# An inverse stored transposed, a gelu moved to its own projection, and deeper weight tiles in a hybrid encoder block

## The chip, the cores and the metric

The kernel runs on one core of a Trainium2 chip. A time is the device time of one execution in microseconds (us). The kernel before was run three times: 1186.85, 1188.13 and 1191.43 us, median 1188.13 us.

The core has engines with a queue each that they work through in order: TensorE (PE, matmuls and its weight loads), VectorE (DVE), ScalarE (ACT), GpSimd (POOL) and SyncE (SP, which only starts transfers here). They wait for each other through semaphores.

## The reference, cut to what matters

One layer of an encoder over 512 tokens with 1024 channels, all in float32: a norm, one wide projection, three branches that mix along the tokens, their gated sum, an output projection with a residual, and an MLP with squared relu between two more norms.

```python
h = rms_norm(x, norm1_g);  p = h @ w_in
y_a = b_a * causal_dwconv(c_a * x_a, conv_a_w)
u   = causal_dwconv(x_b, lru_conv_w, lru_conv_b)
y_b = rg_lru(u, ...) * gelu(g_b)                       # gelu in its tanh form
y_c = rwkv7_recurrence(r, decay, k, v, kk, a) ...      # 16 heads of 64, by token
m   = gate_a * y_a + gate_b * y_b + gate_c * y_c
x   = x + m @ w_out
x   = x + square(relu(rms_norm(x, norm2_g) @ mlp_w1)) @ mlp_w2
return rms_norm(x, final_g)
```

The recurrence of the third branch is worked in chunks of 64 tokens. For that, the inverse of a unit triangular 64x64 matrix is needed for each head and chunk: 16 x 8 = 128 inverses.

## The kernel before, in words

**Precision and the weight stream.** Each float32 operand of a large matmul is split into a high and a low half (float32r each), and three matmuls give the product: high by high, high by low, low by high (`mm3`, L153 to L155). Weights are streamed: `load_half` brings 128x512 values into a tile `raw` by a transfer on SP's queue, ACT casts them to `whi` (L131), and DVE subtracts that from `raw` into `wlo` (`tt`, recorded at L94). A weight block of 1024 rows is two such halves and feeds 24 matmuls, 12 for each half. There are 3 tiles `raw`, 4 `whi` and 4 `wlo`, so a load waits until a tile's last reader is done. Instructions recorded at L94, L97 and L100 belong to helpers (`tt`, `stt`, `ts2`) that the whole kernel uses; one tells them apart by tiles. The tiles of the work pools are shown by the first letters of their tags (`u1` to `u5` all as `u`, `g1` to `g3` as `g`), since numbers are left out.

**The order.** The third branch goes in four groups of four heads. For each group there is a critical chain: `amat` (products `pA`, masked into `AXt`), `inverse`, `chain` (the chunks one after the other) and `post`. Beside it run two fillers: `ab(q)`, the two other branches for a block of 128 channels (two blocks to a group), and `krv(g + 1)`, the inputs of the next group. `weave` hands out steps of the fillers between the yields of the critical part at fixed rates (`R0`, `P1`, `WPOST`, `R4`, `R5`). A list scheduler then orders the instructions of each engine when the program is built: by priority among those whose inputs and tiles are free by its own clock. The weight stream has the highest offset (`OFF` = 160), the critical chain 150 (`CP`), the inverse's tail 60 (`CPI`); the prologue has 20 and 30. On the chip, each engine then keeps that order.

**The inverse.** The diagonal blocks of 32x32 are inverted on DVE, 64 at a time, one per partition (partitions 64 to 127). Two transposes of 32x32 blocks (L482, one for each diagonal block) bring the masked matrix `AXt` into `la`; the identity is loaded into `xt` by a transfer on POOL's queue (L484). Then 31 steps follow, each a multiply into `tmp` and an add into `xt`, of (31 - s)(s + 1) elements. Both `la` and `xt` lie in the tile `Z`, `tmp` in the tile `dg`. Two more transposes (L499) bring the result into `TT`, also in `Z`, another one (L504) a copy into `dg`. After 16 empty yields, which leave the time to the filler, PE forms the off-diagonal block (`pG` at L509, `pT` at L517).

**The filler `ab(q)`.** It projects xb, gb, gatb and c, computes the gates of the linear recurrence from the convolution of xb (`pga`, `pgi`, which need its halves `uh` and `ul`), then the gelu of gb, the recurrence's scan, and projects x, b and ga. Its tiles `u1` to `u5` and `g1` to `g3` have one buffer each; the gelu's tile shares the tag `u3` with the input gate's, and the scaled gate (`gt`) shares `u5` with what follows the scan.

**Later stages.** The merged tiles of the first six blocks go to DRAM and come back on POOL's queue when the last inverse is done (`open_m`, L799 to L801). Then come the output projection (`acc`), and the MLP, whose first and second products have the stretch from 840 us on nearly to themselves.

Of the kernel before, what the change touches and what calls it, by code (L numbers as in the profile page):

```python
# [18 lines left out]
P = 128  # L19
# priorities of the weight stream, the prologue and the critical steps over what is emitted beside them  # L20
OFF, OFFS, OFFP = 160, 20, 30
CP, CPI, CPP = 150, 60, 30
# empty steps that leave the latency of an inverse, or of a norm, to the filler
NINV, NPOST = 16, 6
# steps of the fillers, and their shares by part of the critical path
N_AB, N_KRV = 28, 24
# [62 lines left out]
def block_kernel(ctx, tc, xt, win, par, mulr, sw, wout, w1, w2, fg, cst, eyes, out):  # L89
# [3 lines left out]
    def tt(o, a, b, op):  # L93
        return v.tensor_tensor(out=o, in0=a, in1=b, op=op)  # L94

    def stt(o, a, s, b, op0, op1):
        return v.scalar_tensor_tensor(out=o, in0=a, scalar=s, in1=b, op0=op0, op1=op1)  # L97
# [12 lines left out]

# [1 line left out]
    ident = cp.tile([P, P], F32, name="ident")  # L112
# [8 lines left out]

# [1 line left out]
    def load_w(src):  # L123
# [3 lines left out]
    def load_half(src, i):  # L127
        raw = wp.tile([P, S], F32, tag="raw", name="raw", bufs=3)
        sy.dma_start(raw, src[:, i * S:(i + 1) * S])
        hi = wp.tile([P, S], F32R, tag="whi", name="whi", bufs=4)  # L130
        ac.copy(hi, raw)  # L131
        lo = wp.tile([P, S], F32R, tag="wlo", name="wlo", bufs=4)
        tt(lo, raw, f(hi), SUB)
        return hi, lo
# [22 lines left out]
    def pin(first, mm):  # L157
        # in the order of the program, behind the matmuls before it
        if first:
            tc.keep_in_program_order(mm)  # L160

    def rsqrt(x, y, t):
        # Newton's steps from a first guess on the exponent; within 2 ulp after the third
        ts2(y.bitcast(I32), x.bitcast(I32), -0.5, RSQ, MUL, ADD)
        for _ in range(3):
            tt(t, x, y, MUL)
            stt(t, t, -0.5, y, MUL, MUL)
            stt(y, t, 1.5, y, ADD, MUL)

    def rsqrt_rows(pool, o, ps, low, scale=1.0):  # L170
        # rows alike in each 32: tokens to partitions, the root there, and back
        w = pool.tile([P, S], F32, tag="rqw", name="rqw")
        q = pool.tile([P, 3, 16], F32, tag="rqq", name="rqq")
        v.transpose(w, ps)
        wv = w.rearrange("p (b j) -> p b j", j=32)[:, :, 0]
        if scale == 1.0:
            v.tensor_scalar(out=q[:, 0], in0=wv, scalar1=low, scalar2=None, op0=MAX)
        else:
            ts2(q[:, 0], wv, scale, low, MUL, ADD)
        rsqrt(q[:, 0], q[:, 1], q[:, 2])  # L180
        v.transpose(o, q[:, 1].unsqueeze(2).to_broadcast([P, 16, 32]))

    # =======================================================================
    # projections and the three branches
    # =======================================================================
    ht_ctx = ExitStack()
# [102 lines left out]
    def W(tag, bufs=1):  # L289
        return wk.tile([P, S], F32, tag=tag, name=tag, bufs=bufs)  # L290
# [3 lines left out]

    # low-rank inputs, and the first key tile, on x before its norm's scale
    def unscaled(t, tag):
# [8 lines left out]

    # derived per-channel values
    # sigmoid(z) = (1 + tanh(z / 2)) / 2 throughout: tanh shares its table with exp
    for i, (n, c) in enumerate((("mu_k", -1.0), ("mu_r", -1.0), ("ka", -0.5), ("mu_v", -1.0))):
# [28 lines left out]

    # softplus of the recurrence's parameter
    apv = part[:, PI["ap"]]
# [32 lines left out]
    def krv(g, G_):  # L372
# [5 lines left out]
        for jj in range(2):  # L378
# [50 lines left out]
            tt(G_.BK[:, jj, :, 1], c3(kp), c3(pinv), MUL)  # L429
            # by head: the two tiles' halves side by side  # L430
            if jj == 0:
# [16 lines left out]
    def amat(G_):  # L448
        # A^T = [b|k]^T [a|r], masked
        G_.AX = sp.tile([P, 4, NC, 2, L], F32, tag="AXt", name="AXt")  # L450
        for jj in range(2):
            for c4 in range(2):
                pts = [pm.tile([P, 4, P], F32, tag="pm", name="pA") for h in range(2)]
                for ci in range(4):
                    c = 4 * c4 + ci
                    for h in range(2):
                        rows = slice(64 * h, 64 * h + 64)
                        pe.matmul(pts[h][:, ci], G_.BK[rows, jj, c], G_.AR[rows, jj, c],  # L458
                                  start=True, stop=True)
                for h in range(2):  # L460
                    tt(G_.AX[:, 2 * h + jj, 4 * c4:4 * c4 + 4].rearrange("p c a t -> p c (a t)"),
                       pts[h], mask.unsqueeze(1).to_broadcast([P, 4, P]), MUL)
                yield
        G_.BKT = sp.tile([P, NC, 2, P], F32, tag="BKT", name="BKT")
        for c2 in range(4):
            pt = pm.tile([P, 4, P], F32, tag="pm", name="pB")
            for i in range(4):
                c, jj = 2 * c2 + i // 2, i % 2
                pe.transpose(pt[:, i], G_.BK[:, jj, c].rearrange("p a t -> p (a t)"), ident)
            ac.copy(G_.BKT[:, 2 * c2:2 * c2 + 2].rearrange("p c j t -> p (c j) t"), pt)  # L470
            yield
        G_.RT = sp.tile([P, 2, NC, L], F32, tag="RT", name="RT")
        ac.copy(G_.RT, G_.AR[:, :, :, 1])

    def inverse(G_):
# [5 lines left out]
        for b in range(2):  # L481
            v.transpose(la[32 * b:32 * b + 32].rearrange("l s t -> l t s"),  # L482
                        AXt[32 * b:32 * b + 32, :, :, 0, 32 * b:32 * b + 32].rearrange("s e c t -> s t (e c)"))
        gp.dma_start(xt.rearrange("l s t -> l (s t)"), eyes)  # L484
        # xt[l, s, t] = X[t, s];  X[t, :] += A[t, s] X[s, :], la[l, s, t] = A[t, s]
        yield
        yield
        for s in range(31):
            n, c = 31 - s, s + 1
            tv = tmp[:, 0:n * c].rearrange("l (c t) -> l c t", c=c)  # L490
            tt(tv, la[:, s, s + 1:32].unsqueeze(1).to_broadcast([64, c, n]),
               xt[:, 0:c, s:s + 1].to_broadcast([64, c, n]), MUL)
            tt(xt[:, 0:c, s + 1:32], xt[:, 0:c, s + 1:32], tv, ADD)
            if s % 2 == 1:
                yield
        TT = Z[0:64].rearrange("p a b c -> p (a b c)").rearrange("p (l t) -> p l t", t=L)
        gp.memset(TT[32:64, :, 0:32], 0.0)
        for b in range(2):
            v.transpose(TT[32 * b:32 * b + 32, :, 32 * b:32 * b + 32].rearrange("s l t -> s t l"),  # L499
                        xt[32 * b:32 * b + 32].rearrange("l s t -> l t s"))  # L500
        for _ in range(NINV):
# [139 lines left out]
    def ab(q):  # L641
        # the recurrent branch, then the convolution's
        px = W("u2")
# [9 lines left out]
        t = yield from proj(("gb", q))  # L653
        ac.copy(gb, t)
        yield
        gt = W("u5")
        t = yield from proj(("gatb", q))
        ac.activation(gt, t, AF.Tanh, bias=pv("mgb", q), scale=0.5)
        stt(gt, gt, 1.0, gb, ADD, MUL)
        yield  # L660
        cs = W("g1")
# [15 lines left out]
        ac.activation(ga, ga, AF.Tanh, scale=dvp(P4, q), bias=dvp(P4, q))  # L677
        g2 = W("u3")
        ac.activation(g2, gb, AF.Square)
        ac.activation(g2, g2, AF.Copy, scale=0.044715, bias=1.0)  # L680
        tt(g2, g2, gb, MUL)
        ac.activation(g2, g2, AF.Tanh, scale=0.5 * GELU_C)
        stt(gb, g2, 1.0, gt, ADD, MUL)
        a2 = W("u5")
# [93 lines left out]
    for g in range(NG - 1):  # L778
        fl = fill_main(g)
        # steps of the two fillers, spread over 31 + 24 + 10 steps of the critical part  # L780
        nab = 2 * N_AB - (21 * R0 if g == 0 else 0)
        r2 = ((1 - P1) * nab + N_KRV) / (24 + 10 * WPOST)
        segments([(chainit(amat(GS[g]), inverse(GS[g])), P1 * nab / 31), (chain(GS[g], 0, NC), r2),
                  (post(g, GS[g]), WPOST * r2)], fl)
        drain(fl)

# [1 line left out]
    G_ = GS[NG - 1]  # L788
# [96 lines left out]

    # =======================================================================
    # MLP; the second norm's scale goes to its end
    # =======================================================================
    NA = 3 * NF // 4
    with tc.tile_pool(name="mw", bufs=2) as mw, \  # L890
# [34 lines left out]
        gp.memset(epst, EPS)  # L925
        # the square of the second norm's scale, by token
        sc2 = cp.tile([P, 4], F32, name="sc2")
# [127 lines left out]
```

## Time and profile before

| | |
|---|---|
| Runs | 1186.85, 1188.13, 1191.43 us |
| Profiled execution, span from first to last instruction | 1188.4 us |
| Mean granted TensorE clock | 0.985 |
| PE busy (modelled), matmuls | 1155.3 us (97%), 6396 |
| DVE busy, instructions | 786.9 us (66%), 1537 |
| ACT busy, instructions | 550.5 us (46%), 1005 |
| POOL busy, instructions | 59.2 us (5%), 99 |
| DVE's splits of weights (`wlo`) | 340 of 695 ns, 235.4 us |
| The inverse's 248 steps on DVE | 84.4 us |
| The chain that ended last | PE 84%, DVE 12% |

A row of instructions shows the start, the length, the engine, the line, the operation, the tiles it writes and reads, and the shapes; in brackets, the engine's idle time before it and what ended that. In a row of waits stand who waited, for whom, the total, the count and the longest. Matmuls overlap: the next starts before the one before it has ended, so the distance of their starts is their price. A granted clock of 0.50 means that PE ran at half speed.

### The profile page before, as it was taken

Reading aid. Unit: us, or ns where it says so; the run is one execution under the profiler, and the core shown is the slowest. Engines: PE = TensorE matmul, PEld = TensorE weight load, DVE = VectorE, ACT = ScalarE, POOL = GpSimd, SP = SyncE. Lnnn points to the kernel's source line nnn. Section 1 sums busy time; section 2 is a strip of 40 time slices with the busy share of each in tenths; the row PEclk is TensorE's granted clock in tenths of the full one; section 3 lists DMA queues with packets and bytes.
Section 4 is the critical chain, followed back from the end, with each engine's and each line's share of the span. In section 5 each row is a group of like instructions: output and inputs, shape, how many; then the busy total and the mean of one; then the engine's idle time right before and its main releaser. Section 6 shows DMA issues by size and latency. Waiting matters only on the chain.

```text
span 1188.4 us, 17270 instructions
## 1 busy us (share of the span) xinstructions
PE 1155.3 (97%) x6396; PEld 896.6 (75%) x6396; DVE 786.9 (66%) x1537; ACT 550.5 (46%) x1005; POOL 59.2 (5%) x99
## 2 busy tenths in 40 slices
PE   8999989999999999989999989999999999999996
PEld 4677876677777677767677766889888888888885
DVE  7997985689975678985688975677544444222225
ACT  6655364444556443565444545556444443222224
POOL 4100000000000000000000011000000000000003
PEclk9899988999999999999999999999999999999999
DMA  5231230222332122233122244436323333433322
GB/s 183 89 89 54 89 98 28 63 85 71 96 114 72 41 80 80 85 106 90 46 80 67 71 126 150 151 116 187 124 90 98 89 98 118 154 101 91 105 89 98
DMA packets 61973, 114.69 MB, mean 97 GB/s; under 512 B 7232, under 2 KB 10816, under 8 KB 61888
## 3 DMA queue, kind: packets, MB, share of 16 engines
q1 hardware_dynamic: 54960, 95.49, 26.2%
q0 software_dynamic: 6352, 17.30, 4.6%
q8 instruction: 50, 0.82, 0.3%
q10 hardware_dynamic: 576, 0.79, 0.2%
q14 instruction: 35, 0.29, 0.1%
HBM read 104.64 MB, written 8.91 MB: 96 GB/s over the span
## 4 chain that ended last, share of the span: by engine, by line
PE 84%; DVE 12%; issue 2%; ACT 1%; DMA 0%; SPq 0%; DVEq 0%; ACTq 0%
PE pp L153 12%; PE pp L155 11%; PE pp L154 11%; PE acc L153 6%; PE acc L154 6%; PE acc L155 6%; PE p L155 5%; PE p L153 5%; PE p L154 5%; DVE wlo L94 3%; PE py L582 2%; PE pA L458 2%; PE py L584 2%; DVE Z L94 2%; DVE dg L94 2%
## 5 line engine op out<-in xcount | busy, mean ns | idle before, releaser
L94 DVE TENSOR_TENSOR wlo<-raw,whi 128x512 fp32r<-128x512 f32 x340 | 235.4, 695 | 250.6 <-ACT whi L131 241.7
L131 ACT CAST whi<-raw 128x512 fp32r<-128x512 f32 x340 | 209.7, 619 | 379.1 <-PE acc L155 124.5
L155 PE MATMUL pp<-hh,wlo 128*128 128x512 f32 x696 | 284.4, 410 | 14.8 <-DVE wlo L94 14.5
L153 PE MATMUL pp<-hh,whi 128*128 128x512 f32 x696 | 285.0, 412 | 1.3 <-ACT hh L254 1.3
L154 PE MATMUL pp<-hl,whi 128*128 128x512 f32 x696 | 282.1, 407 | 3.1 <-DVE hl L97 3.1
L155 PEld LDWEIGHTS pp<-hh,wlo 128*128 128x128 f32 x696 | 133.2, 191 | 53.1 <-DVE wlo L94 21.6
L153 PEld LDWEIGHTS pp<-hh,whi 128*128 128x128 f32 x696 | 133.2, 191 | 34.6 <-issue 1.9
L154 PEld LDWEIGHTS pp<-hl,whi 128*128 128x128 f32 x696 | 133.4, 192 | 33.6 <-DVE hl L97 3.7
L155 PE MATMUL p<-h2h,wlo 128*128 128x512 f32 (+1 forms) x264 | 103.0, 390 | 0.1
L153 PE MATMUL p<-h2h,whi 128*128 128x512 f32 (+1 forms) x264 | 103.0, 390 | 0.0
L154 PE MATMUL p<-h2l,whi 128*128 128x512 f32 (+1 forms) x264 | 102.8, 389 | 0.0
L154 PE MATMUL acc<-wlo,ah 128*128 128x512 f32 x256 | 99.7, 390 | 0.0
L155 PE MATMUL acc<-whi,al 128*128 128x512 f32 x256 | 99.6, 389 | 0.0
L153 PE MATMUL acc<-whi,ah 128*128 128x512 f32 x256 | 99.6, 389 | 0.0
L155 PEld LDWEIGHTS p<-h2h,wlo 128*128 128x128 f32 x264 | 49.7, 188 | 11.6 <-DVE wlo L94 0.3
L154 PEld LDWEIGHTS p<-h2l,whi 128*128 128x128 f32 x264 | 49.7, 188 | 11.3
L153 PEld LDWEIGHTS p<-h2h,whi 128*128 128x128 f32 x264 | 49.7, 188 | 11.3
L154 PEld LDWEIGHTS acc<-wlo,ah 128*128 128x128 f32 x256 | 48.1, 188 | 10.1 <-DVE wlo L94 0.3
L153 PEld LDWEIGHTS acc<-whi,ah 128*128 128x128 f32 x256 | 48.1, 188 | 10.1
L155 PEld LDWEIGHTS acc<-whi,al 128*128 128x128 f32 x256 | 48.1, 188 | 10.0
L94 DVE TENSOR_TENSOR Z<-Z,dg 64x31 f32<-64x31 f32 (+15 forms) x124 | 42.2, 340 | 4.1
L94 DVE TENSOR_TENSOR dg<-Z 64x31 f32<-64x31 f32 (+15 forms) x124 | 42.2, 340 | 4.1
(299 smaller groups left out, 1591.3 us busy)
## 6 DMA issues: line engine op xcount, KB each, us to landing
raw<-in_win SPq DMA_DIRECT2D x180, 256.0 KB, 2.6
raw<-in_w SPq DMA_DIRECT2D x128, 256.0 KB, 2.7
raw<-in_wout SPq DMA_DIRECT2D x32, 256.0 KB, 2.6
swr<-in_sw SPq DMA_DIRECT2D x16, 128.0 KB, 2.1
x2T<-in_xt POOLq DMA_DIRECT2D x4, 512.0 KB, 7.1
x2d<-st POOLq DMA_DIRECT2D x8, 256.0 KB, 2.8
xr<-x2d POOLq DMA_DIRECT2D x1, 2048.0 KB, 8.7
xT<-in_xt SPq DMA_DIRECT2D x3, 512.0 KB, 6.8
```

What stands on the lines that cost most here:

```text
L94: return v.tensor_tensor(out=o, in0=a, in1=b, op=op)
L131: ac.copy(hi, raw)
L153: pe.matmul(ps, wh, xh, start=start, stop=False)
L154: pe.matmul(ps, wh, xl, start=False, stop=False)
L155: pe.matmul(ps, wl, xh, start=False, stop=stop)
L458: pe.matmul(pts[h][:, ci], G_.BK[rows, jj, c], G_.AR[rows, jj, c], start=True, stop=True)
L582: pe.matmul(o, RT[64 * h:64 * h + 64, jj, c], St[64 * h:64 * h + 64, jj], start=True, stop=False)
L584: pe.matmul(o, AXt[:, 2 * h + jj, c, 1], sv[:, 2 * h + jj], start=St is None, stop=True)
```

## The change

There are four parts.

- `load_half` has 4 tiles `raw`, 6 `whi` and 6 `wlo`, which is 10 KB more in each partition. The scratch for the descriptors of POOL's transfers is set to 4096 bytes of each partition.
- `la` and `xt` are stored with the row index outside: `la[l, t, s]` and `xt[l, t, s]` in place of `[l, s, t]`. The steps' views exchange their two extents: what ran over (c, n) runs over (n, c). In the two transposes at L482 the destination is now dense, and in the two at L499 the source; the other sides are as before.
- In `ab`, the gelu's three activations and two DVE instructions move from behind the gates to the projections of gb and gatb. Its square reads the projection in PSUM where it read the copy in SBUF.
- Comments are dropped (left out below).

```diff
-        raw = wp.tile([P, S], F32, tag="raw", name="raw", bufs=3)
+        raw = wp.tile([P, S], F32, tag="raw", name="raw", bufs=4)
...
-        hi = wp.tile([P, S], F32R, tag="whi", name="whi", bufs=4)
+        hi = wp.tile([P, S], F32R, tag="whi", name="whi", bufs=6)
...
-        lo = wp.tile([P, S], F32R, tag="wlo", name="wlo", bufs=4)
+        lo = wp.tile([P, S], F32R, tag="wlo", name="wlo", bufs=6)
...
-            v.transpose(la[32 * b:32 * b + 32].rearrange("l s t -> l t s"),
+            v.transpose(la[32 * b:32 * b + 32],
                         AXt[32 * b:32 * b + 32, :, :, 0, 32 * b:32 * b + 32].rearrange("s e c t -> s t (e c)"))
-        gp.dma_start(xt.rearrange("l s t -> l (s t)"), eyes)
+        gp.dma_start(xt.rearrange("l t s -> l (t s)"), eyes)
...
         for s in range(31):
             n, c = 31 - s, s + 1
-            tv = tmp[:, 0:n * c].rearrange("l (c t) -> l c t", c=c)
-            tt(tv, la[:, s, s + 1:32].unsqueeze(1).to_broadcast([64, c, n]),
-               xt[:, 0:c, s:s + 1].to_broadcast([64, c, n]), MUL)
-            tt(xt[:, 0:c, s + 1:32], xt[:, 0:c, s + 1:32], tv, ADD)
+            tv = tmp[:, 0:n * c].rearrange("l (t c) -> l t c", c=c)
+            tt(tv, la[:, s + 1:32, s:s + 1].to_broadcast([64, n, c]),
+               xt[:, s, 0:c].unsqueeze(1).to_broadcast([64, n, c]), MUL)
+            tt(xt[:, s + 1:32, 0:c], xt[:, s + 1:32, 0:c], tv, ADD)
...
             v.transpose(TT[32 * b:32 * b + 32, :, 32 * b:32 * b + 32].rearrange("s l t -> s t l"),
-                        xt[32 * b:32 * b + 32].rearrange("l s t -> l t s"))
+                        xt[32 * b:32 * b + 32])
...
         gb = W("g2")
         t = yield from proj(("gb", q))
         ac.copy(gb, t)
+        g2 = W("u3")
+        ac.activation(g2, t, AF.Square)
+        ac.activation(g2, g2, AF.Copy, scale=0.044715, bias=1.0)
+        tt(g2, g2, gb, MUL)
+        ac.activation(g2, g2, AF.Tanh, scale=0.5 * GELU_C)
         yield
         gt = W("u5")
         t = yield from proj(("gatb", q))
         ac.activation(gt, t, AF.Tanh, bias=pv("mgb", q), scale=0.5)
         stt(gt, gt, 1.0, gb, ADD, MUL)
+        stt(gb, g2, 1.0, gt, ADD, MUL)
         yield
...
         ac.activation(ga, ga, AF.Tanh, scale=dvp(P4, q), bias=dvp(P4, q))
-        g2 = W("u3")
-        ac.activation(g2, gb, AF.Square)
-        ac.activation(g2, g2, AF.Copy, scale=0.044715, bias=1.0)
-        tt(g2, g2, gb, MUL)
-        ac.activation(g2, g2, AF.Tanh, scale=0.5 * GELU_C)
-        stt(gb, g2, 1.0, gt, ADD, MUL)
         a2 = W("u5")
...
-    nc = bacc.Bacc("TRN2", target_bir_lowering=False, num_devices=1)
+    nc = bacc.Bacc("TRN2", target_bir_lowering=False, num_devices=1, dynamic_dma_scratch_size=4096)
```

## The prediction

> **What bounds the kernel now.** I read the page first, then the busy time by stretches, the waits, and the timeline of single engines at the longest waits.
>
> ```profile
> PE 1155.3 (97%) x6396; PEld 896.6 (75%) x6396; DVE 786.9 (66%) x1537; ACT 550.5 (46%) x1005; POOL 59.2 (5%) x99
> ...
> DVE  7997985689975678985688975677544444222225
> ...
> PEclk9899988999999999999999999999999999999999
> ```
>
> TensorE (PE) sets the end, but its 97% is modelled: matmuls overlap, so I price them by the spacing of their starts. VectorE (DVE) averages 66%, yet it has four stretches at 8 or 9 tenths, one for each inverse.
>
> ```profile
> 840.00:1160.00 320.00, 320.00 (x1390) 261.00 (x1389) 118.14 (x175) 105.15 (x175) 1.29 (x2) 1.00 0.33 103
> 157.40:161.10 3.70, 0.42 (x2) 0.00 (x0) 3.67 (x5) 1.70 (x3) 0.00 (x0) 0.88 0.00 0
> 161.10:167.00 5.90, 5.90 (x14) 4.64 (x15) 5.15 (x8) 5.07 (x9) 0.03 (x1) 0.50 0.36 94
> 262.00:274.00 12.00, 12.00 (x88) 9.24 (x87) 9.76 (x17) 3.44 (x6) 1.10 (x2) 1.00 0.34 111
> 274.00:327.50 53.50, 52.84 (x227) 41.31 (x226) 50.43 (x100) 26.87 (x45) 1.72 (x4) 1.00 0.29 84
> 327.50:330.50 3.00, 0.41 (x2) 0.00 (x0) 2.94 (x4) 0.62 (x1) 0.00 (x0) 1.00 0.17 53
> 511.20:514.20 3.00, 0.43 (x2) 0.00 (x0) 2.94 (x4) 0.62 (x1) 0.00 (x0) 1.00 0.18 55
> 692.90:696.60 3.70, 0.39 (x2) 0.00 (x0) 3.64 (x4) 1.26 (x3) 0.00 (x0) 0.93 0.23 71
> 696.60:704.70 8.10, 8.03 (x29) 6.17 (x29) 7.93 (x13) 3.44 (x6) 0.54 (x1) 0.82 0.49 163
> ```
>
> Columns: stretch, its length, busy PE, weight load, DVE, ACT, POOL, granted clock, DMA. In the MLP a matmul costs 320/1390 = 0.23 us; nothing there can gain. In each inverse PE stands still about 3 us while DVE is busy all of it (2.94 of 3.00). DVE was already full before: 50.43 us and 100 instructions, with some 0.03 us between two, fill the 53.5 us.
>
> ```profile
> PE pp L155 <- DVE wlo L94: 14.5, 10, 3.4
> ```
>
> ```profile
> 327.51 0.40 PE L154 MATMUL pp<-hl,whi 128*128 128x512 f32 x1
> 330.58 0.57 PE L155 MATMUL pp<-hh,wlo 128*128 128x512 f32 x1 [2.67 <-DVE wlo L94]
> ...
> 334.33 0.39 PE L155 MATMUL pp<-hh,wlo 128*128 128x512 f32 x1
> ...
> 337.36 0.39 PE L153 MATMUL pga<-uh,swbh 128*128 128x512 f32 x1
> ```
>
> All these waits are for wlo, the low half of a weight split: 14.5 us in ten. A wait shown as 2.67 delays the next start by 3.07 - 0.23 = 2.84 us, so I add 0.17 to each: 16.2 us. By group: 3.70 - 0.42 + 0.17 = 3.4 in the first; 2.84 and the 0.66 + 0.34 before it, 3.8, in the second; the third is its copy; 5.2 are left for the last. Behind each long wait the clock is at half: 14 matmuls in 5.90 us where 3.2 would do (2.7 lost); nine starts from 330.58 to 334.33 instead of 2.07 us (1.7 lost, three times). That is 7.8 more. **The ceiling of the change is 16.2 + 7.8 = 24 us.**
>
> **The change, part by part.** *Deeper tiles.* The late split stands behind the two closing transposes:
>
> ```profile
> 325.77 4.03 DVE L499 STREAM_TRANSPOSE Z<-Z 32x1024 f32<-32x1024 f32 x2
> 329.84 0.69 DVE L94 TENSOR_TENSOR wlo<-raw,whi 128x512 fp32r<-128x512 f32 x1
> ...
> 331.11 1.23 DVE L504 STREAM_TRANSPOSE dg<-Z 32x1024 f32<-32x1024 f32 x1
> ...
> 335.09 0.69 DVE L94 TENSOR_TENSOR ul<-u,uh 128x512 fp32r<-128x512 f32 x1
> ...
> 343.19 0.69 DVE L94 TENSOR_TENSOR u<-u,g 128x512 f32<-128x512 f32 x1
> ```
>
> A half feeds 12 matmuls, 2.8 us. Two more of each tile let the stream, which has the highest priority, run two halves or 5.6 us further ahead, more than any of these waits. The splits are no more in number; two (1.4 us) are made ahead of the full stretch, where DVE idles 12.00 - 9.76 = 2.2 us, and two more stand ahead of everything later: zero within it. The fourth raw tile only starts loads earlier. So waits for wlo go: -16.2 and -7.8, unless something else is late next.
>
> *Transposes.* Per inverse two at L482 and two at L499.
>
> ```profile
> L482 DVE STREAM_TRANSPOSE Z<-AXt 32x1024 f32<-32x1024 f32 x8 | 16.6, 2080 | 0.2
> L499 DVE STREAM_TRANSPOSE Z<-Z 32x1024 f32<-32x1024 f32 x8 | 16.0, 1999 | 0.3
> L504 DVE STREAM_TRANSPOSE dg<-Z 32x1024 f32<-32x1024 f32 x4 | 4.9, 1226 | 0.0
> ```
>
> L504, with dense rows on both sides, takes 1.23 us for the same 1024 elements. After the change L482 writes densely but still reads AXt 512 B apart; L499 reads densely and writes Z 256 B apart. No row has a transpose with one dense side. The nearest are the inverse's first and last step, 31 elements each, dense and 128 B apart:
>
> ```profile
> 113.10 0.19 DVE L94 TENSOR_TENSOR dg<-Z 64x31 f32<-64x31 f32 x1
> ...
> 154.01 0.22 DVE L94 TENSOR_TENSOR dg<-Z 64x31 f32<-64x31 f32 x1
> 154.26 0.21 DVE L94 TENSOR_TENSOR Z<-Z,dg 64x31 f32<-64x31 f32 x1
> ```
>
> The multiply at 154.01 reads strided and writes densely: 0.03/31 = about 1 ns an element, the transposes' own surplus (0.77 to 0.85 us over 1024). The add at 154.26 strides on both sides and pays no more. So I take reads as what costs: L482 keeps 2.08, L499 falls to 1.23, saving 2 x 0.77 = 1.5 us an inverse. Bounds: 0 and 1.5 + 1.7 = 3.2. The 62 step instructions have the same sizes with the two extents exchanged (the strided step becomes the first): zero. The identity's load on POOL's queue is the same transfer.
>
> [...]
>
> *The gelu.* Its two DVE instructions (0.69 each) and three activations move two projections earlier in each of eight tiles; no count changes, and the square reads PSUM. In the middle groups the first tile's stay inside the full stretch; the second tile's multiply (343.19, after the stretch) may come before ul at 335.09: +0.7. In the first group, whose second tile began earlier, both do: +1.4. On ACT the square no longer waits for a shared tile:
>
> ```profile
> 298.03 0.63 ACT L679 ACTIVATE u<-g 128x512 f32<-128x512 f32 x1 [3.47 <-DVE u L97]
> 298.57 0.60 ACT L131 CAST whi<-raw 128x512 fp32r<-128x512 f32 x1
> ```
>
> The high-half cast queued behind it could come up to 3.5 us earlier; while DVE is the later one I count zero. Against that, the gelu's tanh now waits at its new place for its multiply on DVE, with the gate's tanh and high-half casts queued behind it, and splits and PE behind those: some 2 to 4 us by the row above, within the 5.6 us of the two spare halves. If that cover is gone, it is a wait of up to 3.5 us.
>
> *The smaller descriptor scratch.* POOL's queue carries few transfers; its densest burst reloads the merged tiles.
>
> ```profile
> mh<-mhd POOLq DMA_DIRECT2D x5, 256.0 KB, 4.8
> ```
>
> ```profile
> 710.58 0.54 POOL L799 DMA_DIRECT2D mh<-mhd  x1 [11.93 <-ACT AXt L521]
> ```
>
> ```profile
> 757.23 0.28 PE L153 MATMUL acc<-mh,whi 128*128 128x256 f32 x1
> ```
>
> Ten such transfers, each only after the one before had landed, would end at about 710.6 + 10 x 5 = 761, 4 us late; a gain is excluded, since nothing waits for room now. Issued one behind the other as now, 0.54 us each, they land by 710.6 + 5.4 + 4.8 = 721, 36 us early: zero.
>
> *Prologue.* The deeper stream also acts here.
>
> ```profile
> 29.17 1.76 DVE L94 TENSOR_TENSOR wlo<-raw,whi 128x512 fp32r<-128x512 f32 x1
> 30.85 2.40 DVE L97 SCALAR_TENSOR_TENSOR hl<-xT,n1t,hh 128x512 fp32r<-128x512 f32 x2
> ```
>
> PE waits for the first hl. The split ahead of it can move off (-1.8), or two more can come in front (+3.5); I take zero.
>
> **What is late next.** In the second group the gate product at 337.36 needs ul, done at 335.78. Without waits and half clock PE would be there at 337.36 - 3.8 - 1.7 = 331.9; ul would be done at 335.8 - 1.5 + 0.7 = 335.0. So 3.1 us of the wait return, with 1.7 of half clock: 0.7 saved, and the same in the third group. In the first and last group the next need is the product on L504's result.
>
> ```profile
> 159.25 1.23 DVE L504 STREAM_TRANSPOSE dg<-Z 32x1024 f32<-32x1024 f32 x1
> ...
> 160.98 0.67 DVE L94 TENSOR_TENSOR u<-u,g 128x512 f32<-128x512 f32 x1
> ...
> 698.40 1.23 DVE L504 STREAM_TRANSPOSE dg<-Z 32x1024 f32<-32x1024 f32 x1
> ```
>
> ```profile
> 169.11 2.21 PE L509 MATMUL pG<-dg,AXt 32*32 32x32 f32 x64
> ...
> 704.70 1.19 PE L509 MATMUL pG<-dg,AXt 32*32 32x32 f32 x32
> ```
>
> The multiply at 160.98 is the gelu's of the first group's second tile, now behind L504; it and its combine move ahead. First group: PE arrives at 169.1 - 3.4 - 2.7 = 163.0; L504 ends at 160.5 - 1.5 + 1.4 + 1.4 (two splits before it) = 161.8: all 6.1 saved. Last: PE at 704.7 - 5.2 - 1.7 = 697.8, L504 done at 699.6 - 1.5 = 698.1: 6.9 - 0.3 = 6.6. **Sum: -6.1 - 0.7 - 0.7 - 6.6 = -14.1.** The profiled execution's span is 1188.4 us, 0.3 from the median of the runs, 1188.13, so nothing around it is added: 1174.
>
> **The rivals.** *All four transposes become dense* (3.2): ul at 333.3, wait 1.4, too short for the half clock that followed waits near 3; 4.1 in each middle group, 6.1 and 6.9 outside: 21.2, 1167. For it: only the both-sided case is known slow for a transpose. Against: the row at 154.01.
>
> *No transpose gains* (0): middle groups ul at 336.5, 5.5 - 4.6 - 1.7 = -0.8 each; first 5.8 (163.3 against 163.0), last 6.9 - 1.8 = 5.1: 9.3, 1179. For it: 154.01 read as any strided side.
>
> *The deeper tiles stay unused*, so the change doesn't do what it says: the high-half cast, stuck in ACT's queue as at 298.57, comes too late to fill them. Then only 1.5 - 0.7 = 0.8 a group remains: 3.2, 1185. Against: while DVE has no idle time, a cast that is 3.5 us late is seldom what its split waits for, since other work stands before the split on DVE anyway.
>
> *Slower: DVE's total decides, not its order.* If the second tile's two gelu instructions (1.4) and the two extra splits (1.4) all fall inside each full stretch, it grows by 2.8 less what the transposes save, four times, on top of today's waits: 4 x 2.8 = 11.2, 1200, with no saving; 4 x 1.3, 1194, with 1.5. It decides from a saving under 2.8. For it: DVE is full for 53 us. Against: 2.2 us of idle time just before, and the second tile's combine also needs the gate's projection, which ends after the stretch in the middle groups.
>
> **How the numbers follow.** Forecast 1174 (own range 1169 to 1179) 0.41; all dense, 1167, 0.17; none dense, 1179, 0.16; unused, 1185, 0.13; slower, 0.13. A measurement of this kernel tells about 0.5%, 5.9 us, from no change. Below 1182.2 lie nearly all of the first two, most of the third and a little of the fourth: 0.71. Unchanged: the rest of these, 0.16. Slower: 0.13. The range for eight in ten leaves out the far end of the dense case and of the slower one: 1163 to 1192.
>
> **What would show it.** Right: no wait of pp L155 on wlo near 3 us in the inverses, L499 near 1.23 and L482 near 2.08, waits on ul or half clocks in the middle groups. Wrong: wlo waits of the same 14.5 us (tiles unused); L499 unchanged; a longer hl wait in the prologue; a stretch of DVE longer than today's 53.5 us, for which the slower case stands.

## The result, and the profile after

The changed kernel takes 1194.85 us (median of 11 runs, 1192.06 to 1198.60) against 1188.13 us for the kernel before: 1.0055 times as long, 95% interval 1.0038 to 1.0072. It is slower by 6.7 us, where 14 us less had been predicted.

The waits of PE in the changed kernel (who waited, for whom, total, count, longest):

```profile
PE pga L153 <- ACT uh L148: 8.2, 2, 4.1
PE pp L154 <- DVE hl L97: 4.6, 2, 4.3
PE pT L517 <- ACT dg L511: 3.2, 1, 3.2
PE pp L153 <- ACT xgh L228: 2.7, 1, 2.7
PE pG L509 <- DVE dg L504: 1.8, 1, 1.8
...
PE pga L153 <- ACT dg L511: 1.0, 1, 1.0
```

The ten waits for `wlo`, 14.5 us, are gone. In their place are two of 4.1 us for `uh` (groups 2 and 3), one of 3.2 for the copy `dg` in the first group, two in the last, and longer ones in the prologue. All rows of the view add up to 22.9 us before and 25.4 after: the waits moved, and grew a little.

What they cost beside that stands in the columns of a view by stretches (length, busy PE with its matmuls, weight load, DVE, ACT, POOL, granted clock, DMA). For the second group, from its first `pA` to its first `pV` (the inverse), and from there to the next `pA` (the chain), before:

```profile
261.60:365.60 104.00, 100.66 (x563) 79.29 (x562) 87.47 (x153) 54.39 (x87) 4.54 (x10) 0.98 0.33 98
365.60:445.30 79.70, 79.70 (x531) 55.41 (x529) 55.38 (x136) 38.25 (x84) 1.70 (x4) 1.00 0.20 58
```

and after, with the wait for `uh` and the 6.8 us behind it:

```profile
262.50:367.10 104.60, 100.49 (x556) 79.93 (x555) 86.01 (x151) 52.74 (x85) 4.53 (x10) 0.97 0.30 92
367.10:448.30 81.20, 81.20 (x537) 56.11 (x537) 56.15 (x137) 39.08 (x86) 1.70 (x4) 1.00 0.20 63
332.10:336.10 4.00, 0.18 (x1) 0.00 (x0) 4.00 (x6) 2.61 (x5) 0.12 (x1) 1.00 0.58 187
336.10:342.90 6.80, 6.51 (x15) 4.87 (x16) 5.08 (x9) 6.17 (x11) 0.00 (x0) 0.50 0.45 155
```

The inverse has 7 matmuls less and takes 0.6 us more. The chain got them and takes 1.5 us more. So the group loses 2.0 us: two starts of PE (331.89 and 336.39) lie 4.27 us further apart than the usual 0.23, where there were 3.8 of that in all, and 6.8 us are at half clock where there were 3.4. DVE did not get more to do in the inverse (86.01 us, 151 instructions, against 87.47 and 153).

In the same two profiles the prologue takes 1.7 us more and the third group 1.3 more, while the first and the last group take 0.8 less each and all that follows 1.3 less.

So the two profiled executions differ by 2.1 us only (spans 1190.5 and 1188.4), the medians by 6.7. What the medians have beyond that goes with the clock: the changed kernel's runs have a median granted clock of 0.980, the kernel before 0.986 in the runs beside the experiments. That is 2 x 0.020 x 1193 = 48 us at half speed against 33, and 15 us more at half speed cost up to 7.5. The profiled execution, with 0.982, is one of the better ones.

Why `uh` is late, from DVE's timeline, before and after:

```profile
325.05 0.69 DVE L94 TENSOR_TENSOR ul<-g,uh 128x512 fp32r<-128x512 f32 x1
325.77 4.03 DVE L499 STREAM_TRANSPOSE Z<-Z 32x1024 f32<-32x1024 f32 x2
329.84 0.69 DVE L94 TENSOR_TENSOR wlo<-raw,whi 128x512 fp32r<-128x512 f32 x1
...
332.84 1.51 DVE L97 SCALAR_TENSOR_TENSOR u<-u,part,u 128x510 f32<-128x510 f32 x2
334.27 0.68 DVE L94 TENSOR_TENSOR wlo<-raw,whi 128x512 fp32r<-128x512 f32 x1
335.09 0.69 DVE L94 TENSOR_TENSOR ul<-u,uh 128x512 fp32r<-128x512 f32 x1
```

```profile
326.01 4.06 DVE L499 STREAM_TRANSPOSE Z<-Z 32x1024 f32<-32x1024 f32 x2
330.10 0.69 DVE L94 TENSOR_TENSOR wlo<-raw,whi 128x512 fp32r<-128x512 f32 x1
330.71 0.69 DVE L94 TENSOR_TENSOR ul<-g,uh 128x512 fp32r<-128x512 f32 x1
...
334.36 0.67 DVE L94 TENSOR_TENSOR u<-u,g 128x512 f32<-128x512 f32 x1
334.96 0.73 DVE L97 SCALAR_TENSOR_TENSOR u<-u,part,u 128x509 f32<-128x509 f32 x1
335.62 0.67 DVE L94 TENSOR_TENSOR wlo<-raw,whi 128x512 fp32r<-128x512 f32 x1
336.37 0.69 DVE L94 TENSOR_TENSOR ul<-u,uh 128x512 fp32r<-128x512 f32 x1
```

DVE is full in both: from 274.0 us before and from 275.0 us after to the end of the second tile's `ul` it works 59.2 of 62.5 us and 58.9 of 62.1 us. In the changed kernel the first tile's `ul` (330.71) and the gelu's multiply (334.36) stand between the transposes and the second tile's `ul` (336.37), where they did not before, and three splits are still between. From the group's first `pA` to there DVE makes 19 splits of weights, where it was 20. So the second tile's halves are ready 74.6 us after the group's first `pA`, where it was 74.2 before, and PE, no longer held up by `wlo`, stands 4.1 us at `pga`. The transposes did not help:

```profile
L482 DVE STREAM_TRANSPOSE Z<-AXt 32x1024 f32<-32x1024 f32 x8 | 16.1, 2011 | 0.2
L499 DVE STREAM_TRANSPOSE Z<-Z 32x1024 f32<-32x1024 f32 x8 | 16.1, 2011 | 0.3
```

They took 2080 and 1999 ns. One dense side is worth 0.07 us at L482 and nothing at L499. Where the tiles are alike (number 2 below against the kernel before, by the medians) it is worth 0.08 us at L482 (2002 ns after 2080) and 0.04 us at L499 (1976 after 2016), of some 0.8.

### The profile page after: what moved, and what is told of

Its sections match the earlier page's. It is cut to its first block, busy times and chain, and to the rows that moved or that the text cites. A ratio compares the mean times of both kernels' runs of the same rounds, so it can differ in the third digit from the quotient of the medians.

```text
span 1190.5 us, 17254 instructions
## 1 busy us (share of the span) xinstructions
PE 1155.3 (97%) x6396; PEld 898.1 (75%) x6396; DVE 785.1 (66%) x1537; ACT 547.7 (46%) x1005; POOL 59.7 (5%) x99
## 4 chain that ended last, share of the span: by engine, by line
PE 84%; DVE 12%; issue 2%; ACT 2%; DMA 0%; SPq 0%; DVEq 0%; ACTq 0%
PE pp L154 12%; PE pp L153 11%; PE pp L155 11%; PE acc L153 6%; PE acc L154 6%; PE acc L155 6%; PE p L153 5%; PE p L155 5%; PE p L154 5%; DVE wlo L94 3%; PE py L582 2%; PE py L584 2%; PE pA L458 2%; DVE Z L94 1%; DVE dg L94 1%
## 5 line engine op out<-in xcount | busy, mean ns | idle before, releaser
L154 PE MATMUL pp<-hl,whi 128*128 128x512 f32 x696 | 285.5, 410 | 4.6 <-DVE hl L97 4.6
```

Of the source, the lines that this page charges most:

```text
L154: pe.matmul(ps, wh, xl, start=False, stop=False)
```

## The experiments

Ratios are to the kernel before on the same chip, with 95% intervals.

### 1 to 3: the parts alone

Theory A says that DVE's total in the stretch decides and that deeper tiles only move waits; rival B that the early gelu is what costs.

```diff
# 1: before, with the tiles and the scratch alone
-        raw = wp.tile([P, S], F32, tag="raw", name="raw", bufs=3)
+        raw = wp.tile([P, S], F32, tag="raw", name="raw", bufs=4)
... (whi and wlo: bufs=6; dynamic_dma_scratch_size=4096)
# 2: before, with the layout of la and xt alone (L482 to L499 of the change)
# 3: before, with the gelu's five instructions moved alone
```

> The kernel before with the deeper tiles (4 raw, 6 + 6 split) and the smaller descriptor scratch alone. Theory A (VectorE's total work in an inverse's stretch sets the time; deeper tiles only move TensorE's wait from the split wlo to the next thing VectorE is late with): no waits on wlo in the inverses, waits of 3 to 4.5 us on uh or on the inverse's products in their place, 1187 to 1193 us. Theory B (the deeper tiles gain as predicted, and the gelu's new place loses it again): 1174 to 1181 us.

> The kernel before with the inverse's storage alone changed. Theory A (a strided side costs whichever side it is): L482 and L499 stay at 2.0 us, no measurable change, 1186 to 1190 us. The predicted mechanism (only reads cost): L499 near 1.23 us and some 1.5 us less in each stretch, 1181 to 1185 us.

> The kernel before with the gelu moved alone. Theory A: 0.7 to 1.4 us more VectorE work inside each stretch, so 0 to 4 us slower, 1188 to 1192 us. Theory B (the gelu's place is what costs): 1194 to 1200 us. If the shorter waits in ScalarE's queue matter: 1182 to 1187 us.

Tiles alone: 1197.12 us, ratio 1.0071 (1.0051 to 1.0090). Layout alone: 1185.06, 0.9969 (0.9956 to 0.9982). Gelu alone: 1189.82, 1.0019 (0.9996 to 1.0042). The tiles alone lose as much as the whole change (the two intervals overlap), with nearly the same waits as the changed kernel:

```profile
PE pga L153 <- ACT uh L148: 8.1, 2, 4.1
...
PE pT L517 <- ACT dg L511: 4.4, 1, 4.4
...
PE pG L509 <- DVE dg L504: 1.8, 1, 1.8
...
PE pp L155 <- DVE wlo L94: 0.3, 1, 0.3
```

So rival B falls: `uh` is late without the gelu's move. Theory A has the waits right (25.3 us in all, 22.9 before) and the time too low (1187 to 1193). In this profile the two middle inverses are 0.8 us shorter than before, with 7 matmuls less each, and the chains behind them 4.4 and 2.9 us longer, of which those matmuls are 1.5, as in the changed kernel. The rest stands in windows of 6.8 and 3.4 us at half clock, which begin 1.4 and 1.8 us behind the chain's first `pV`, without a wait of PE before them. So the loss is in part not behind any wait.

The layout's time is below theory A's (1186 to 1190) and at the edge of the predicted mechanism's (1181 to 1185), but it comes without transposes near 1.23 us (medians of 2002 and 1976 ns); its runs have a median clock of 0.990 beside 0.986 or 0.987 for the kernel before, some 8 us less at half speed, and that can be all of the 3 us. The gelu alone is undecided: its runs spread from 1182 to 1198 us, and the profiled one shows why (stretches within the first group's chain):

```profile
176.30:213.80 37.50, 37.50 (x190) 23.57 (x187) 14.24 (x41) 11.91 (x31) 0.00 (x0) 0.50 0.06 19
213.80:251.30 37.50, 37.50 (x250) 25.47 (x249) 26.04 (x63) 17.41 (x38) 1.70 (x4) 1.00 0.19 57
```

There the clock stayed at half for 37.5 us without any wait of PE.

### 4 and 6: DVE relieved, with six and with four tiles

Number 4 is the changed kernel with all four transposes dense on both sides, by permuted blocks, so that the inverses are those of other matrices and the output is not the layer's; number 6 the same with 4+4 tiles, 3 `raw` and the scratch of before.

```diff
-  AXt[32 * b:32 * b + 32, :, :, 0, 32 * b:32 * b + 32].rearrange("s e c t -> s t (e c)"))
+  AXt[32 * b:32 * b + 32, :, :, 0, 32 * b:32 * b + 32].rearrange("s e c t -> s (e c) t"))
...
-  v.transpose(TT[32 * b:32 * b + 32, :, 32 * b:32 * b + 32].rearrange("s l t -> s t l"),
+  v.transpose(TT[32 * b:32 * b + 32, :, 32 * b:32 * b + 32],
```

> The changed kernel with the two strided sides of the inverse's transposes read and written in rows of 32 neighbours (the same elements in another order: the output is not the reference's, since the inverse's matrices are permuted). It takes 4 x 0.8 = 3.2 us from VectorE in each inverse and nothing else. Theory A: the moved waits of 4.3 us shrink to about 1, the half clock behind them goes, 1172 to 1181 us. Rival C (the waits are set by the order of ScalarE's queue or by the scheduler's order, not by VectorE's total): the waits stay, 1190 to 1196 us.

> The same kernel (4+4 split tiles) with each inverse's four strided transposes reading and writing rows of 32 neighbours (1.23 us each and not 2.0; the blocks then hold permuted matrices, so the output is not the reference's). With six tiles this took 1177.6 us. Theory A (tiles only move waits while DVE is full, but pay when it has room): 4+4 tiles are slower than 1177.6 here, 1180 to 1184, with waits for wlo of 6 to 9 us. Rival C (tiles cost whatever room DVE has, because their splits go ahead of other work in ACT's and DVE's order): 4+4 tiles are faster, 1171 to 1176, about 7 us under the six-tile one, as without dense transposes.

Six tiles: 1177.59 us, ratio 0.9921 (0.9900 to 0.9941). Four tiles: 1173.37 us, 0.9904 (0.9868 to 0.9940). The dense transposes take 1237 and 1234 ns, 3.1 us less DVE in each inverse, and the whole is 17 us shorter than the changed kernel. With six tiles the waits for `uh` and for `wlo` read:

```profile
PE pga L153 <- ACT uh L148: 2.0, 2, 1.0
```

and with four:

```profile
PE pp L155 <- DVE wlo L94: 4.7, 3, 2.6
```

The wait for `uh` falls by 3.1 us in each middle group, one for one with what DVE was relieved of. That is theory A's mechanism. Its forecast for number 6, that six tiles pay once DVE has room (1180 to 1184 with four), is wrong: four are not slower. The time lies where rival C had it (1171 to 1176), but the two intervals overlap, and three of number 6's ten runs took 1185.6 to 1186.8 us.

### 5 and 7: the change without the tiles; the scratch alone

```diff
# 5: the changed kernel with raw 3, whi 4, wlo 4, scratch as before
# 7: before, with
+    nc = bacc.Bacc("TRN2", target_bir_lowering=False, num_devices=1, dynamic_dma_scratch_size=4096)
```

> The changed kernel with one part undone: 3 raw and 4+4 split tiles and the descriptor ring as before; layout and gelu as changed. Theory A (the six tiles put splits ahead of other work on full engines, and are the whole loss): the two other parts alone were -3.0 and +1.7 us against the kernel before, so some 1187 us (1184 to 1190); PE's waits for wlo back at 12 to 14 us in about ten, waits of pga for uh under 1.5, pp's wait for hl in the prologue under 2. Rival B (the parts only cost together: the gelu's earlier ACT and DVE work and the new layout leave no room, tiles or not): 1192 to 1196, with waits of pga for uh of 4 us or more.

> The kernel before with the descriptor ring of 4096 alone. Theory A: no change, 1187 to 1190 us, POOL's DMAs issue and land as before. Rival D (the smaller ring holds POOL's DMA issues up, and it, not the tiles, is the cause of the 9 us that tiles and ring lost together): 1194 to 1198.

Number 5: 1185.38 us, 0.9966 (0.9952 to 0.9981). Number 7: 1187.78 us, 0.9988 (0.9972 to 1.0003). The scratch does nothing that can be told; the tiles cost about 9 us, with the other parts (1194.85 less 1185.38) or without them (number 1). Theory A's time (1184 to 1190) came; of its signs the wait for `hl`, under 2 us, did not. Number 5's waits and its second group:

```profile
PE pp L155 <- DVE wlo L94: 12.7, 8, 3.9
PE pp L154 <- DVE hl L97: 3.1, 1, 3.1
...
PE pT L517 <- ACT dg L511: 1.1, 1, 1.1
```

```profile
257.90:361.60 103.70, 100.40 (x563) 79.33 (x562) 86.90 (x153) 54.21 (x87) 4.53 (x10) 0.98 0.31 98
361.60:441.30 79.70, 79.70 (x531) 55.43 (x529) 55.35 (x136) 38.27 (x84) 1.72 (x4) 1.00 0.19 58
```

The two stretches take 183.4 us, as before (183.7). What number 5's profile gains, 4.8 us, lies for the most part in the first group, whose chain had no half clock in this execution (79.8 us after 82.7).

### 8: the chain of u ahead of the splits

```diff
+        with tc.high_priority(offset=150):
             ac.copy(px, t)
             ...
             uh, ul = split(wk, u, "u")
```

> The changed kernel with the chain of u (copy, convolution, split into uh and ul) planned ahead of the weight splits, so that the waits of pga for uh (8.2 us in two) go. Theory A (engines are full; a wait that is taken away comes back elsewhere): pga's waits under 2 us, but waits for wlo, pT's or pG's operands rise by as much; 1191 to 1196. Rival E (only a bad place in the order: DVE and ACT have slack in the inverse of the middle groups): both waits of 4.3 us and the half clock that follows them (6.8 us each, so 3.4 lost each) go, 15 us less: 1179 to 1183; if only the waits go, 1186.

1198.46 us, 1.0074 (1.0053 to 1.0095).

```profile
PE pga L154 <- DVE ul L94: 5.3, 2, 2.7
...
PE pga L153 <- ACT uh L148: 4.7, 2, 2.3
PE pG L509 <- DVE dg L504: 3.1, 1, 3.1
```

`pga` waits 10.0 us (5.3 + 4.7) and not 8.2, in two pieces each, and the product on L504's result 1.3 us longer. Rival E, a bad place in the order alone, falls. Theory A missed too: it had the waits at `pga` go and come back elsewhere, and they stayed; its time was 1191 to 1196.

### 9: the strided side given to ACT

```diff
-            v.transpose(la[32 * b:32 * b + 32], AXt[...].rearrange("s e c t -> s t (e c)"))
+            ac.copy(dg[r].rearrange("s t (e c) -> s e c t", c=NC), AXt[r, :, :, 0, r])
+            v.transpose(la[r], dg[r])
...
+            v.transpose(dg[r], xt[r])
+            ac.copy(TT[r, :, r], dg[r].rearrange("s t l -> s l t"))
```

> The kernel with 4+4 split tiles, new layout and early gelu (1185.4 us), where ACT copies each block of A into a staging tile by neighbours ahead of the first transposes, and out of one behind the last, so that DVE's four transposes are dense in both sides and the result is the reference's. ACT gets four copies of 1024 elements, some 1.05 us each by L521's 2.09 for two. Theory A (DVE's total in the stretch sets the end, ACT has room): 3.2 us of DVE less in each inverse, four transposes near 1.23 us, and the time near that of the dense case with permuted matrices: 1172 to 1178. Rival F (ACT's queue is as full: the copies delay casts, uh or dg): 1182 to 1188, with waits of PE for what ACT writes.

1192.49 us, 1.0041 (1.0014 to 1.0069); the profile is of its longest run, 1205.48 us. The transposes are dense now (1237 and 1236 ns), but ACT's copies cost twice what was expected, and DVE stands behind them:

```profile
L483 ACT COPY dg<-AXt x8: 2004/2070/2092, 109.9 to 659.0; 32x1024 f32<-32x1024 f32 x8
```

```profile
  DVE Z L484: 11.7, 8
```

(The first row: shortest, median and longest in ns; the second: who waited for it, us and times.) DVE gains 0.77 us a transpose and waits 1.5 us for each copy at L483. Neither theory named that wait, and both missed the time. Rival F's sign, waits of PE for what ACT writes, came: 3.3 us in four for `BKT`, which ACT copies.

### 10 and 11: later splits; three raw tiles

```diff
# 10: the changed kernel; projections' loads from the first chain on
-        w = load_w(win[CN[name]])
+        w = load_w(win[CN[name]], offw[0])      # 60 in place of OFF = 160
# 11: the changed kernel
-        raw = wp.tile([P, S], F32, tag="raw", name="raw", bufs=4)
+        raw = wp.tile([P, S], F32, tag="raw", name="raw", bufs=3)
```

> The changed kernel with the weight splits of the projections planned 60 steps ahead and not 160, from the first group's chain on; the tiles are unchanged. Theory A' (the six tiles are kept full, so a full stretch of DVE has as many splits in it as with four; if the splits come later, the two spare halves drain in the stretch): DVE and ACT do up to two splits less in each inverse (1.4 us and 1.2 us), pga's waits for uh fall from 4.1 to 2.7 or less, and half clocks with them: 1185 to 1191. Rival G (the order of splits does not matter, since work behind them waits as much): 1193 to 1197, waits for uh near 4 or for wlo in their place.

> The changed kernel with 3 raw tiles in place of 4, the split tiles 6+6. Theory H (the fourth raw tile starts a weight transfer and its cast and split earlier in the prologue, ahead of xgl, hl on DVE and xgh on ACT): the prologue's end comes 1 to 2 us earlier than the changed kernel's 98.3, the wait for hl is 3.1 and not 4.4, 1193 us; nothing else changes. Rival I (the fourth raw tile is also what fills the six split tiles in the stretch): waits for uh under 2 and for wlo back at 12 us, 1186 to 1189.

Number 10: 1196.53 us, 1.0076 (1.0049 to 1.0103); number 11: 1194.82 us, 1.0049 (1.0031 to 1.0066). In number 10 one split less stands in the stretch (18) and the waits for `uh` fall to 6.5 us in two, the longest 3.3 where A' had 2.7 or less; the median clock falls to 0.976, and A' fails on the time. Number 11 can't be told from the changed kernel (1194.85): I fails, and the fourth `raw` tile does nothing that can be told. H fails too: the prologue ends no earlier (99.3 us, 98.3 in the changed kernel, 96.7 before), and its waits for `hl` add up to 5.0 us (4.6 in the changed kernel). All profiles with 4+4 split tiles have one of 3.1 there, so this wait grows with `whi` and `wlo`. The prologue's end does not tell the tiles apart: number 5, with 4+4, has it at 98.9 us.

### 12 and 14: the waits filled

So far the waits grew by 2.5 us, and the time at half clock, by the median clocks, by 15. Theory J: the half clock comes because PE stands still for long. Rival K: it comes with something else. Number 14 fills the two waits for `uh` with matmuls that achieve nothing; number 12 fills also that for `dg` in the first group.

```diff
+    def busy(ps, w, x, n):
+        for i in range(n):
+            pin(i == 0, pe.matmul(ps, w, x, start=True, stop=True))
...
         pga = pm.tile([P, S], F32, tag="pm", name="pga")
+        busy(pga, bd, hh[:, 0], {1: 16, 3: 16}.get(q, 0))
         mm3(pga, swh[:, 0], swl[:, 0], uh, ul)
# 12 also: 12 into pT's tile ahead of pT, first group
```

> The changed kernel with idle matmuls in three of its long waits: 16 of 128x512 (0.235 us each, 3.8 us) into pga's own tile ahead of pga in the second tile of the groups 2 and 3, where PE waits 4.3 us for uh, and 12 into pT's tile in the first group, where it waits 3.3 us for dg; the real matmuls overwrite them. PE gets nothing done earlier by them. Theory J (the half clock follows PE's stretches without work, and the change's whole loss is the half clock): the windows at 175.7 (10.2 us), 336.1 (6.8) and 520.4 (6.8) go, up to 12 us less: 1183 to 1189. Rival K (the half clock has another cause, or follows the restart whatever ran before): no gain, 1194 to 1198, windows as before in the same places.

> The changed kernel with the idle matmuls ahead of pga alone (16 in each middle group's second tile), without those ahead of pT, which in the run before could not start until the wait was over and so added 3.3 us to the first group. Theory J, with what that run showed for the two middle inverses (104.6 to 102.0 and 103.9 to 102.0 us): 4.5 us less than the changed kernel, 1190 to 1191, with no half clock between 330 and 345 and between 515 and 530. Rival K: 1194 or more.

Number 12: 1193.32 us, 1.0032 (1.0019 to 1.0046). The twelve ahead of `pT` could not start, because their tile was what ACT's copy still had to free:

```profile
173.59 4.61 PE L164 MATMUL pT<-hh,bd 128*128 128x512 f32 x12 [3.13 <-ACT dg L519]
```

so they came on top, and the time lies between J's range (1183 to 1189) and K's (1194 to 1198). Number 14, without them: 1190.76 us, 1.0026 (1.0001 to 1.0050), where 1190 to 1191 was expected. Its matmuls from 331 to 344 us and its second group's inverse:

```profile
L164 PE MATMUL pga<-hh,bd 128*128 128x512 f32 x16 | 3.9, 396 | 0.0
L153 PE MATMUL pga<-uh,swbh 128*128 128x512 f32 x1 | 0.5, 505 | 0.3 <-ACT uh L148 0.3
```

```profile
264.50:366.50 102.00, 101.43 (x572) 80.83 (x571) 85.78 (x151) 52.42 (x85) 4.53 (x10) 1.00 0.31 95
```

The clock is 1.00 all through, the inverse takes 102.0 and not 104.6 us, the third group's 101.9 and not 103.9. PE got no result earlier; only the 6.8 us at half speed behind each wait are gone. In the profiles this is shown twice for each of two groups, so theory J holds behind these waits. In the time it is 4.1 us, but there the intervals of numbers 14 and the changed kernel (to 1.0050 and from 1.0038) still overlap.

### 13: the same in the kernel with four tiles

```diff
+            if kt == 0 and name in (("c", 1), ("c", 3)):
+                busy(t, wh, hh[:, 0], 11)
```

> The kernel with 4+4 tiles, new layout and early gelu (1185.4 us), with 11 such idle matmuls (2.6 us) ahead of the projection of c in the second tile of the groups 2 and 3, where PE waits 3.0 us for wlo and 3.4 us of half clock follow. Theory J: both windows go, 1.7 us each: 1181 to 1184. Rival K: 1185 to 1188.

1184.11 us, 0.9965 (0.9942 to 0.9989). Both windows go; the inverses take 102.7 and 102.6 us where 103.7 and 103.6 stood, so 1 us each and not 1.7. The time is at the upper end of J's range (1181 to 1184) and can't be told from number 5's. Numbers 2, 5 and 13 are all faster than both kernels by their intervals, and not told apart from each other.

## Why the prediction was wrong, step by step

**The ceiling, 16.2 us of waits and 7.8 of half clock: found.** The `wlo` waits were there and went. But it counted only the half clock behind long waits; the kernel before has 33 us of it by its median clock, and the changed one 48.

**Deeper tiles, "zero within it": the step that failed first.** The tiles were used and all `wlo` waits went, as said. What was wrong is that this takes waiting time off PE. DVE is full in the stretch, all but one of the splits still stand on it (19 for 20), and PE waits for whatever comes out last. Number 1 shows it: tiles alone, all but 0.3 of the 14.5 us of `wlo` gone, 25.3 us of waits in all for 22.9, and 9 us lost.

**Transposes, 1.5 us an inverse: wrong, 0.1 to 0.25 us.** "Reads are what costs" was read from one multiply at 154.01. After the change L499 reads densely and takes 2.01 us all the same: a strided write pays as much. With one dense side L482 and L499 take 2011 and 2011 ns, with two 1237 and 1234 (number 4).

**What is late next.** For the middle groups the step named the right instruction, the second tile's `ul` and `uh` before `pga`, and was off in two terms. It had 3.1 us come back, with 1.5 less for the transposes and 0.7 more for the gelu; without the 1.5 that is 4.6, and 4.27 came. And it had 1.7 us for the half clock, where 3.4 were lost (6.8 us at half). So the saving of 0.7 became the loss of 2.0 that the second group shows.

For the first and the last group the step stopped too early on the path: at `pG`, which needs L504's result. Up to there it was right. In the first group `pG` starts 66.2 us after the group's first `pA` (forecast 66.4, before 72.5). But the next need is ACT's copy of `pG` into `dg`, ahead of `pT`. Before:

```profile
174.85 0.58 ACT L511 COPY dg<-pG 32x512 f32<-32x512 f32 x1
177.04 1.89 PE L517 MATMUL pT<-Z,dg 32*32 32x32 f32 x54
```

and after:

```profile
169.95 1.28 ACT L710 ACT_TABLE_LOAD   x1 [0.16 <-DVE g L97]
171.25 0.69 ACT L710 ACTIVATE g<-pp,part 128x512 f32<-128x512 f32 x1
171.83 2.09 ACT L521 COPY AXt<-AR 64x1024 f32<-64x1024 f32 x2
173.93 1.05 ACT L511 COPY dg<-pG 32x512 f32<-32x512 f32 x2
175.04 2.68 PE L517 MATMUL pT<-Z,dg 32*32 32x32 f32 x54 [3.17 <-ACT dg L511]
```

PE reached `pT` at 171.7 and stood until 175.0 behind a table load, an activation and two copies. By the group's first `pA`, `pG` came 6.3 us earlier than before, ACT's copy 2.1 and `pT` 3.7; a window of 10.2 us at half clock followed, and of the 6.1 us forecast the whole group keeps 0.8. I followed DVE's queue there and not ACT's. For the last group, `pG` starts 5.1 us earlier by the first `pA`, after a wait of 1.8 us for L504 (forecast 6.6, or 5.1 if no transpose gains). Behind it stand a piece of 3.4 us at half clock, a wait of 1.0 us of `pga` for ACT's copy `dg`, and another piece: its inverse takes 85.2 us after 86.1.

**The gelu, +0.7 and +1.4 of DVE: about right.** Its multiply stands ahead of `ul` as foreseen (334.36). Alone it is 1.0019 with an interval across 1, and leaving it in costs nothing measurable (number 5 against 2).

**Scratch, zero: right** (number 7). **Prologue, zero: wrong within its bounds** of -1.8 and +3.5. The first `pA` comes 1.7 us later. PE's longest wait for `hl` is 4.3 us and not 3.1, since two splits, and not one, precede the first `hl`; that the rest of the 1.7 us is the tiles' doing is not shown (number 5):

```profile
30.00 1.78 DVE L94 TENSOR_TENSOR wlo<-raw,whi 128x512 fp32r<-128x512 f32 x1
...
33.37 1.75 DVE L94 TENSOR_TENSOR wlo<-raw,whi 128x512 fp32r<-128x512 f32 x1
35.05 2.73 DVE L97 SCALAR_TENSOR_TENSOR hl<-xT,n1t,hh 128x512 fp32r<-128x512 f32 x4
```

**The rivals.** The time fell into the slower rival's span (1194 to 1200; by its own terms, 5.2 and 11.2 us above 1188.1, it is 1193.3 to 1199.3), but its mechanism, two gelu instructions and two more splits within a longer stretch on top of today's waits, is not what happened: DVE's work in the inverse did not grow, and the `wlo` waits went. Its title, that DVE's total decides and not its order, fits numbers 4 and 8. "No transpose gains" was true of the transposes within 0.08 us each, and its 1179 us was not, since it kept the first and last group's savings. "All dense" falls with the 2011 ns, and "the deeper tiles stay unused" with the `wlo` waits that went.

**Left open.** Why the same total of waits brings more half clock with six tiles. Part of it is settled: two of its windows are due to the two waits for `uh` (numbers 12 and 14). But in six of 16 chains of the middle groups with six tiles a window came without a wait, and in one of 14 with four (number 9, with its copies on ACT, not counted). In each of the six chains a window begins 1.0 to 2.3 us behind the first `pV`. Four tiles do not keep it away: in the first group's chain it came so in four of seven profiles with four tiles (before, 3, 6 and 7). Nothing here tells why.

## What to carry to other kernels

More buffers took nothing off an engine that was full (DVE made 19 splits in the stretch where it made 20, and the tiles cost 9 us): ask which instruction on it the waiting engine needs last, in every queue that this passes, before a wait is booked as saved. A wait of some 3 us or more on TensorE cost in these profiles what it lasted and mostly a further 1.7 to 5.1 us of half clock (windows of 3.4 to 10.2); where it can't be removed, matmuls without use that fill it gave most of that back in the profiles (numbers 12 to 14), if the tile that they write is free when the wait begins. For a transpose of 32x1024 elements on DVE, one strided side cost about as much as two, whichever side it was: 2011 ns at both lines with one, 2080 and 1999 with two, 1237 and 1234 with none.

## What the runs showed of the hardware

In the profiles here the granted clock stands at half for 3.41 us or a multiple of it: 3.4, 6.8, 10.2, 13.7, and once each 34.1 (number 9) and 37.5 (number 3). The stretch that the end of the execution falls into is apart (6.2 us in the record before, 6.9 in that of the changed kernel). In the 16 profiles behind the first 12 us, I compared each distance of two starts of PE with the usual one of that kind of matmul. Where it was longer by 2.6 us or more, a window followed within 4.5 us in 55 of 56 cases; by 1.6 to 2.6 us, in 10 of 19; by 0.9 to 1.6 us, in 12 of 35. But 11 of these 12 stand within 6 us of a longer one; of the 22 that stand alone one was followed by a window. Of the 56, nine stand in the profiles before and after, each with a window. How long the window gets does not go by the distance: 3.54 us more was followed by 3.4 us at half clock (before, last group), 3.34 us by 10.2 and 4.27 us by 6.8 (the changed kernel, first and second group). Why, is not shown. Not expected were the windows in the chains, where PE is never without an instruction, but many of its matmuls are small (`pu`, 64x64 by 64x64; number 3: 190 matmuls in 37.5 us at half clock, 250 at full). They come in some executions of one kernel and not in others: the runs of number 3 go from 1182 us at a clock of 0.991 to 1198 at 0.973.

A strided copy on ACT took as long as DVE's transposes with a strided side: 2.07 us for 32x1024 elements written 128 B apart (L483 of number 9), where a copy of 64x1024 by rows of 64 neighbours takes half of 2.09.
